# Neighbourhood attention in an encoder layer: key chunks of 16 columns moved by 8, two for each query block

## The chip, the cores and the metric

The kernel runs on one core of one Trainium2 chip. Its time is the device time of one execution in microseconds (us). The time before is the median of three runs.

A core has five engines that run side by side, each with its own instruction stream: TensorE (PE in the profile; its weight loads stand apart as PEld), VectorE (DVE), ScalarE (ACT), GpSimd (POOL) and SyncE (SP). They wait for each other through semaphores. TensorE computes `out = weights^T @ moving`: a weight load brings 128 x 128 values into the array, and a matmul streams the columns of the moving operand past them and adds into a bank of PSUM of 128 x 512 float32 values.

## What is computed

One encoder layer on 512 tokens of width 2048, in float32. One projection gives queries, keys, values and gates for 32 heads of 64 dimensions. Sixteen heads (group A) do dilated sliding-window attention, which the change leaves alone. Sixteen heads (group B) do neighbourhood attention. Both are gated, concatenated, projected, added to the residual and normalised.

For group B the 512 tokens are a grid of 8 rows by 64 columns. With 8 rows the window covers all of them, and along the columns it is 16 wide, around the query and clamped at the grid's edges:

```
q_start = np.clip(qcol - NA_COLS // 2, 0, GRID_W - NA_COLS)
col_mask = (kcol >= q_start[:, :, None]) & (kcol < q_start[:, :, None] + NA_COLS)
bias = jnp.where(col_mask[:, None, :, None, :], bias, NEG_INF)
s = jnp.einsum('bhrqd,bhrkd->bhrqk', q_blk, k_blk).astype(jnp.float32) * scale + bias_blk[None]
p = jax.nn.softmax(s, axis=-1)
return jnp.einsum('bhrqk,bhrkd->bhrqd', p, v_blk.astype(jnp.float32))
```

Queries are taken in four blocks of 16 columns (128 queries with the 8 rows). The queries of columns 0 to 15 need key columns 0 to 23; those of 16 to 31 need 8 to 39; those of 32 to 47 need 24 to 55; those of 48 to 63 need 40 to 63.

## The kernel before, in words

**Precision.** Each float32 operand is split into a high part and a low remainder (ACT writes the high part, DVE subtracts), and a product is made of two or three matmuls that add into one bank.

**Stages.** First come six gate products and the splitting of the input. Then six blocks of Strassen products give keys, queries and values of both groups, which are stored in DRAM. While these run, POOL builds the tables of biases in DRAM (`prep_heads` for group A, `prep_b` for group B, there the learned bias and the column mask together). Then comes the attention stage (in the profile about 561 to 900 us), and last the rest of the output projection with the normalisation.

**The attention stage** is one loop of 136 steps whose order on PE, ACT, DVE and SP is written out by hand; POOL's order is left to a scheduler. Step n belongs to query block n % 4 of head n // 4. Heads come in pairs, pairs of group A and of group B in turn, so eight steps (an octet) are one pair. A step does this:

- `scores(n)` (L548, L549): two matmuls with the block's 128 queries (high part with half of a remainder, then the rest) as weights and the keys as the moving operand. DVE adds the bias and takes the row's extreme (L512, `softmax`), and ACT takes the exponential into a tile `p` (L516). The tiles `p` are a ring of three.
- `turn(n - 2)` (L566): PE transposes the probabilities of two steps before, 128 keys at a time. Each transpose loads 128 columns of `p` as weights and streams an identity of 128 columns. ACT copies the result as the high part `th` (L572), DVE makes the low part `tl` (L573).
- at n % 4 = 2, `values(n // 4 - 1)` (L586): the previous head's probabilities, high and low, are multiplied with its values, for which four chunks of 128 keys lie in the tile `vv`. Then ACT copies one half and DVE adds both (L707, L708).
- between these, `fill` issues a fixed number of matmuls of other work: gate products (L459), and then the first half of the output projection (L635). In all there are 864 of them in the stage, whatever the heads do.

**Group B before.** The values lie in chunks of 16 columns by 8 rows: chunk 0 is columns 0 to 15, and so on. Query block b uses the chunks b - 1, b and b + 1 that exist: two at the edges, three in the middle. So scores are 256 or 384 columns wide, `turn` makes two or three transposes, and `values` runs, for each of `th` and `tl`, over chunk 1 for 384 queries, chunk 2 for 384, chunk 0 for 256 and chunk 3 for 256. For `th` chunk 2 is cut in 128 and 256 queries.

**POOL in the attention stage** issues transfers only: the gate's result (L466), and for each pair the softmax denominators on their way through DRAM (`share`): one write `rc_d` (L601) and, when it has landed, two reads `rc` (L603).

Of the kernel before, what the change touches and what calls it, by code (L numbers as in the profile page):

```python
# [9 lines left out]
AF = mybir.ActivationFunctionType  # L10
# [38 lines left out]
def _col_masks():  # L49
    m = np.full((3, 16, 48), BIG, np.float32)  # L50
    for cq in range(16):
        for v, (q0, k0, w) in enumerate(((0, 0, 32), (16, 0, 48), (48, 32, 32))):
            lo = min(max(q0 + cq - 8, 0), 48)
            for j in range(w):
                if lo <= k0 + j < lo + 16:
                    m[v, cq, j] = 0.0
    return np.ascontiguousarray(np.repeat(m.transpose(1, 0, 2), 8, axis=0))


def _view(t, offset, dims):  # L60
    return bass.AP(tensor=t.tensor, offset=t.offset + offset, ap=dims)
# [2 lines left out]
BLOCKS = (("k", 0), ("q", 0), ("v", 0), ("k", 1), ("q", 1), ("v", 1))  # L64
ORDER = [(m % 2, m // 2) for m in range(2 * PAIRS)]
EARLY = 6
BIAS = ((0, 32), (256, 48), (640, 32))
BW = 896


def hybrid_layer(tc, xT, xn, w_in, w_early, w_gate, w_out, t5x, brow, rpb, cmask, eye, gain, lbias, out):
    nc = tc.nc
    from contextlib import ExitStack
    with ExitStack() as ctx:
# [8 lines left out]
        def f(ap):  # L83
            return ap.bitcast(F32)
# [51 lines left out]
        v_d = [dram.tile([PAIRS, 128, 4, 256], F32, name=f"v{g}_d") for g in range(2)]  # L136
# [24 lines left out]
        def prep_b(g):  # L161

            held = []

            def rows():
                b0 = slot("b0", F32, "rpbs")
                r = b0[:, :720].rearrange("p (d j) -> p d j", d=15)
                masks = b0[:, 720:864].rearrange("p (v j) -> p v j", v=3)
                held.extend((r, masks))
                nc.gpsimd.dma_start(masks, cmask)  # L170
                for c in range(16):
                    nc.gpsimd.dma_start(r[8 * c:8 * c + 8],
                                      _view(rpb, PADB + 8 * g * RPB - 1 + c * (RPBW - 1), [[RPB, 8], [31, 15], [1, 48]]))

            def table(v):
                r, masks = held
                w, o = BIAS[v][1], 16 if v == 0 else 0
                gt = slot("b1", F32, "gt")[:, :15 * w].rearrange("p (d j) -> p d j", d=15)
                nc.gpsimd.tensor_tensor(gt, masks[:, v:v + 1, 0:w].to_broadcast([128, 15, w]), r[:, :, o:o + w],
                                        ALU.subtract)  # L180
                held.append(gt.rearrange("p d j -> p (d j)"))

            def write(v):
                at, w = BIAS[v]
                for k in range(8):
                    nc.gpsimd.dma_start(_view(bias_d[1], (1024 * g + 16 * k) * BW + at, [[BW, 16], [128 * BW, 8], [1, 8 * w]]),
                                      held[2][:, w * (7 - k):w * (7 - k) + 8 * w])
                held.pop()

            def both(v):  # L190
                write(v - 1)
                table(v)

            return [rows, lambda: None, lambda: table(0), lambda: both(1), lambda: both(2), lambda: write(2)]


# [3 lines left out]
        for tag, n, ops in (("s0", 4, A5), ("s1", 4, A5), ("c0", 2, A6), ("c1", 2, A6),  # L200
                            *((f"n{i}", 1, A6) for i in range(4)), *((f"n{i}", 1, A3) for i in range(4, 12))):
            t = slot(tag, F32R, "op").rearrange("p (n s q) -> p n s q", n=n, s=2)
# [286 lines left out]

        def load_v(i):  # L490

            g, j = ORDER[i]
            vv = slot(f"t{4 * (i % 2) + 2}", F32R, "vv").rearrange("p (b e) -> p b e", b=4)
            nc.sync.dma_start(f(vv.rearrange("p b e -> p (b e)")), v_d[g][j].rearrange("p b e -> p (b e)"))
            vs[i] = vv.rearrange("p b (h e) -> p b h e", h=2)

        def load_sg(i):
            sgs[i] = sg_ring.next("sg")
            nc.sync.dma_start(sgs[i], sg_d[i])

        def softmax(sc, bias, n, grp, i, col):

            s = s_ring.next("s")
            p = p_ring.next("p")
            mn = small.tile([128, 1], F32, name="mn", tag="mn")
            if col == 0:
                dens[i] = small.tile([128, 8], F32, name="den", tag="den")
            den = dens[i][:, col:col + 1]
            flat = (s[:, :n], sc[:, :n])
            if grp == 1:  # L510
                flat = (t.rearrange("p (r c) -> p r c", r=8) for t in flat)
            nc.vector.tensor_tensor_reduce(*flat, bias, 1.0, 3e38, ALU.add, ALU.min, mn)  # L512
            order = "p (r b c) -> p b r c"

            def exponent():
                nc.scalar.activation(p[:, :n].rearrange("p (b r c) -> p b r c", r=8, c=16),  # L516
                                     s[:, :n].rearrange(order, r=8, c=16), AF.Exp, bias=mn, scale=-1.0, accum_out=den)
            return p, exponent

        SLOT = ((0, 2), (1, 3, 5), (4, 6, 8), (7, 9))  # L520
        loaded, vs, biases, probs, turned, dens, sgs, yt, rcs = {}, {}, {}, {}, {}, {}, {}, {}, {}

        def head(h):
# [4 lines left out]
        def load_bias(h):  # L528
            g, _, _, hg = head(h)
            bias = ring_b.next("bias")  # L530
            n = BW if g else 560
            nc.sync.dma_start(bias[:, :n], bias_d[g][hg])
            biases[h] = bias

        def scores(n):

            h, b = divmod(n, 4)
            g, i, a, _ = head(h)
            qt, ql, kt = loaded[i]
            cols = slice(128 * b, 128 * b + 128)  # L540
            sc = bank(pss, "sc")
            o, ko = sc, kt[:, a]
            if g:
                rows = "p (r w) -> p r w"
                c0, nch = max(b - 1, 0), 2 if b in (0, 3) else 3
                o = sc[:, :128 * nch].rearrange(rows, r=8)
                ko = ko.rearrange(rows, r=8)[:, :, c0 * 16:(c0 + nch) * 16]
            nc.tensor.matmul(o, qt[:, a, cols], ko, start=True, stop=False)  # L548
            nc.tensor.matmul(o, ql[:, a, cols], ko, start=False, stop=True)  # L549
            if g == 0:  # L550
                p, exponent = softmax(sc, biases[h][:, 48 - 16 * b:560 - 16 * b], 512, 0, i, 4 * a + b)
                probs[n] = p, 4
                return exponent
            at, w = BIAS[(0, 1, 1, 2)[b]]
            p, exponent = softmax(sc, biases[h][:, at:at + 8 * w].rearrange(rows, r=8), 128 * nch, 1, i, 4 * a + b)
            probs[n] = p, nch
            return exponent

        def turn(n):
            h, b = divmod(n, 4)  # L560
            p, nch = probs.pop(n)
            if b == 0:
                turned[h] = slot("s0", F32R, "th"), slot("s1", F32R, "tl")
            pt = bank(pst, "pt").rearrange("p (k q) -> p k q", k=4)
            for k in range(nch):
                nc.tensor.transpose(pt[:, k], p[:, k * 128:k * 128 + 128], ident)  # L566
            if head(h)[0] == 0:
                th, tl = (t.rearrange("p (k q) -> p k q", k=4)[:, :, 128 * b:128 * b + 128] for t in turned[h])
            else:
                s0 = SLOT[b][0]  # L570
                th, tl = (t.rearrange("p (s q) -> p s q", s=16)[:, s0:s0 + 2 * nch - 1:2] for t in turned[h])
            nc.scalar.activation(th, pt[:, :nch], AF.Copy)  # L572
            nc.vector.tensor_tensor(tl, pt[:, :nch], f(th), ALU.subtract)  # L573

        rest = ((0, 0, 256, 0), (3, 256, 512, 8))
        whole = ((1, 0, 384, 2), (2, 128, 512, 5)) + rest
        opening = ((1, 0, 384, 2), (2, 384, 512, 7), (2, 128, 384, 5)) + rest
        full = tuple((k, 0, 512, 4 * k) for k in range(4))

        def values(h):  # L580
            g, i, a, _ = head(h)
            vv = vs[i]
            pv = bank(pss, "pv")
            for m, (src, parts) in enumerate(zip(turned.pop(h), (opening, whole) if g else (full, full))):
                for n, (kc, q0, q1, s) in enumerate(parts):
                    nc.tensor.matmul(pv[:, q0:q1], vv[:, kc, a], src[:, 128 * s:128 * s + q1 - q0],  # L586
                                     start=m == 0 and n == 0, stop=m == 1 and n == 3)
            if a == 0:
                yt[i] = y_ring.next("y")
            me, other = slice(64 * a, 64 * a + 64), slice(64 - 64 * a, 128 - 64 * a)  # L590
            return pv[me], pv[other], yt[i][me], tmp[me]
# [90 lines left out]
        with tc.manual_schedule(engines=engines):  # L682
# [6 lines left out]
            for n in range(136):  # L689
                b, i = n % 4, n // 8  # L690
# [11 lines left out]
                exponent = scores(n) if n < 128 else None  # L702
                if mixing:
                    if exponent:
                        exponent()
                    mine, theirs, y, t = values(n // 4 - 1)
# [28 lines left out]
        for tiles, src, first in ((gb, gain, 0), (bb, lbias, 6)):  # L735
            for i in range(4):
                t = slot(f"n{first + i}", F32, "gain")
# [76 lines left out]
        for dc in (2, 3):  # L814
            for u in range(4, 8):
                raw = out_ring.next("wraw")
                nc.sync.dma_start(raw[:, :1024], w_out[8 * dc + u])
                i = 2 * (u - 4)
                wts[dc, u] = [slot(f"{'tr'[dc - 2]}{i + m}", F32R, "wlast") for m in range(2)]
                split(raw[:, :1024], *wts[dc, u])  # L820
        for t in range(4):
            for dc in (2, 3):
                acc = bank(pacc, "acc") if dc == 2 else bank((pss, pst)[t % 2], "acc")
                parts = (slice(0, 384), slice(384, 512)) if (t, dc) == (3, 3) else (slice(0, 512),)
# [69 lines left out]
```

## Time and profile before

| what | value |
|---|---|
| median of three runs | 996.21 us (996.02 to 996.49) |
| the profiled execution: its time, its span | 997.12 us, 995.3 us |
| PE busy, PEld busy | 981.0 us (99%), 866.9 us (87%) |
| DVE, ACT, POOL busy | 765.9 us (77%), 499.9 us (50%), 208.6 us (21%) |
| mean granted TensorE clock | 0.995 |
| until the first scores, 0 to 561.29 us | PE 558.22, DVE 451.20, ACT 257.00, POOL 168.23 us busy |
| 561.29 to 892.00 us (attention) | PE 330.19, DVE 236.62, ACT 220.43, POOL 29.40 us busy |
| 892.00 to 995.30 us | PE 92.61, DVE 78.09, ACT 22.47, POOL 11.00 us busy |

How it is read: the span is the time from the first to the last instruction of the profiled execution. A matmul's busy time contains its way through the array, so matmuls in a row overlap in the profile; what one costs is the distance from its start to the start of the next. The timeline merges equal instructions that follow each other into one row with their count, and a row that merges several widths names that of the first.

### The profile page before, as it was taken

To read this page: it belongs to the slowest core of one execution; us is meant where nothing else is said; L and a number is where in the kernel's file an instruction comes from. 1 tells how busy PE (TensorE), PEld (TensorE's weight loads), DVE (VectorE), ACT (ScalarE), POOL (GpSimd) and SP (SyncE) were. 2 spreads that over 40 slices of the span, in tenths; PEclk is the share of its full clock that TensorE was granted. 3 is DMA by queue.
4 is the path that set the end of the run, shared out by engine and by line. 5 is a ranking of instruction groups with operands and counts; after the bars stand their busy time and mean duration, and the time that the engine had idled before them with its cause. 6 is when DMAs were issued, how large, how long until landed. Compare 5 with 4: busy or idle time off the path is not lost.

```text
span 995.3 us, 16145 instructions
## 1 busy us (share of the span) xinstructions
PE 981.0 (99%) x5899; PEld 866.9 (87%) x5899; DVE 765.9 (77%) x1146; ACT 499.9 (50%) x839; POOL 208.6 (21%) x322
## 2 busy tenths in 40 slices
PE   9999999999999999999999999999999999999995
PEld 6889999999889999999888888888888888888885
DVE  7958779678888887787987466776776867777876
ACT  6544444345344444434454367666667676773200
POOL 1003655654753730000000001001110001000021
PEclk9999999999999999999999999999999999999998
DMA  9833688698498387439527866677668677668222
GB/s 337 281 120 67 186 282 248 170 286 221 130 280 264 128 247 242 119 105 255 146 65 234 278 196 213 186 230 225 203 184 248 196 226 220 198 212 293 85 75 95
DMA packets 115567, 198.46 MB, mean 199 GB/s; under 512 B 46287, under 2 KB 64207, under 8 KB 115488
## 3 DMA queue, kind: packets, MB, share of 16 engines
q1 hardware_dynamic: 102976, 171.87, 55.5%
q0 software_dynamic: 12512, 25.57, 9.2%
q8 instruction: 46, 0.75, 0.3%
q14 instruction: 33, 0.27, 0.1%
HBM read 150.77 MB, written 46.60 MB: 198 GB/s over the span
## 4 chain that ended last, share of the span: by engine, by line
PE 96%; DVE 1%; ACT 1%; DMA 0%; issue 0%; SPq 0%; ACTq 0%; DVEq 0%
PE acc L635 15%; PE acc L459 11%; PE acc L367 11%; PE acc L365 11%; PE acc L366 11%; PE acc L358 5%; PE acc L359 5%; PE acc L360 5%; PE pv L586 5%; PE pt L566 4%; PE sc L548 2%; PE sc L549 2%; PE acc L267 2%; PE acc L268 2%; PE acc L269 2%; PE sc L635 1%
## 5 line engine op out<-in xcount | busy, mean ns | idle before, releaser
L87 ACT ACTIVATE wh<-braw 128x1024 fp32r<-128x1024 f32 x168 | 178.0, 1060 | 237.0 <-PE acc L366 158.0
L88 DVE TENSOR_TENSOR wl<-braw,wh 128x1024 fp32r<-128x1024 f32 x168 | 206.1, 1229 | 73.8 <-ACT wh L87 72.5
L365 PE MATMUL acc<-xk,wh 128*128 128x256 f32 x512 | 143.6, 282 | 1.1 <-ACT wh L87 1.1
L366 PE MATMUL acc<-xk,wh 128*128 128x256 f32 x512 | 143.5, 282 | 0.0
L367 PE MATMUL acc<-xk,wl 128*128 128x256 f32 x512 | 141.1, 282 | 0.0
L373 DVE TENSOR_TENSOR braw<-braw 128x1024 f32<-128x1024 f32 x96 | 117.3, 1236 | 1.1
L635 PE MATMUL acc<-wh,yk 128*128 128x512 f32 x320 | 108.7, 401 | 0.0
L573 DVE TENSOR_TENSOR tl<-pt,th 128x512 fp32r<-128x512 f32 (+2 forms) x128 | 75.3, 589 | 41.9 <-ACT th L572 40.6
L365 PE MATMUL acc<-op,wh 128*128 128x256 f32 x384 | 107.4, 282 | 0.0
L366 PE MATMUL acc<-op,wh 128*128 128x256 f32 x384 | 107.4, 282 | 0.0
L516 ACT ACTIVATE p<-s,mn 128x512 f32<-128x512 f32 (+2 forms) x128 | 82.0, 640 | 49.0 <-DVE mn L512 48.6
L367 PE MATMUL acc<-op,wl 128*128 128x256 f32 x384 | 105.2, 283 | 0.0
L365 PEld LDWEIGHTS acc<-xk,wh 128*128 128x128 f32 x512 | 97.2, 190 | 1.6 <-ACT wh L87 1.5
L366 PEld LDWEIGHTS acc<-xk,wh 128*128 128x128 f32 x512 | 97.2, 190 | 0.1
L572 ACT ACTIVATE th<-pt 128x512 fp32r<-128x512 f32 (+2 forms) x128 | 65.9, 516 | 60.5 <-PE pt L566 58.9
L367 PEld LDWEIGHTS acc<-xk,wl 128*128 128x128 f32 x512 | 95.8, 190 | 0.0
L459 PE MATMUL acc<-xk,wh 128*128 128x512 f32 x320 | 90.7, 401 | 0.0
L512 DVE CUSTOM_DVE_ANT_0 s<-sc,bias 128x512 f32<-128x512 f32 (+2 forms) x128 | 74.4, 581 | 15.0 <-PE sc L549 14.1
L367 PEld LDWEIGHTS acc<-op,wl 128*128 128x128 f32 x384 | 71.5, 190 | 1.7 <-DVE wl L88 1.7
L365 PEld LDWEIGHTS acc<-op,wh 128*128 128x128 f32 x384 | 73.0, 190 | 0.0
L366 PEld LDWEIGHTS acc<-op,wh 128*128 128x128 f32 x384 | 73.0, 190 | 0.0
L566 PEld LDWEIGHTS pt<-ident,p 128*128 128x128 f32 x416 | 53.1, 140 | 16.1
(156 smaller groups left out, 2058.7 us busy)
## 6 DMA issues: line engine op xcount, KB each, us to landing
braw<-in_w_in SPq DMA_DIRECT2D x96, 512.0 KB, 5.0
wraw<-in_w_out SPq DMA_DIRECT2D x32, 512.0 KB, 6.2
wraw<-in_w_gate SPq DMA_DIRECT2D x20, 512.0 KB, 5.3
k_d<-kst SPq DMA_DIRECT2D x64, 128.0 KB, 4.4
q_d<-kst SPq DMA_DIRECT2D x64, 128.0 KB, 3.5
v_d<-vst SPq DMA_DIRECT2D x32, 256.0 KB, 5.0
q<-q_d SPq DMA_DIRECT2D x32, 256.0 KB, 6.1
k<-k_d SPq DMA_DIRECT2D x16, 512.0 KB, 5.4
```

Of the source, the lines that this page charges most:

```text
L87: nc.scalar.activation(hi, raw, AF.Copy)
L88: nc.vector.tensor_tensor(lo, raw, f(hi), ALU.subtract)
L365: nc.tensor.matmul(o, h[:, c], ah, start=k == 0 and n == 0, stop=False)
L366: nc.tensor.matmul(o, h[:, c], al, start=False, stop=False)
L367: nc.tensor.matmul(o, l[:, c], ah, start=False, stop=k == 7 and n == 1)
L373: nc.vector.tensor_tensor(dst[u], dst[u], other[u], ALU.add)
L459: nc.tensor.matmul(acc, w[:, k * 128:k * 128 + 128], X[8 * u + k][:, s], start=u == 0 and n == 0 and k == 0, stop=u == 1 and n == 2 and k ...
L512: nc.vector.tensor_tensor_reduce(*flat, bias, 1.0, 3e38, ALU.add, ALU.min, mn)
L516: nc.scalar.activation(p[:, :n].rearrange("p (b r c) -> p b r c", r=8, c=16), s[:, :n].rearrange(order, r=8, c=16), AF.Exp, bias=mn, scale ...
L566: nc.tensor.transpose(pt[:, k], p[:, k * 128:k * 128 + 128], ident)
L573: nc.vector.tensor_tensor(tl, pt[:, :nch], f(th), ALU.subtract)
L635: nc.tensor.matmul(acc[:, part], yk[k][:, s, c], w[:, wk], start=first and kk == 0 and n == 0, stop=last and kk == 1 and n == 2)
```

## The change

For group B, the chunks of values now hold 16 columns that begin at column 8: chunk 0 is columns 8 to 23, chunk 1 is 24 to 39, chunk 2 is 40 to 55, and chunk 3 is columns 56 to 63 and 0 to 7. Each query block then needs exactly two chunks. The scores are computed for the columns that the block needs, 24, 32, 32 and 24, which with 8 rows are 192, 256, 256 and 192 columns in place of 256, 384, 384 and 256. At the edges the quarter of `p` that belongs to columns the block doesn't see is set to zero on POOL. The tables of biases shrink with the scores (896 to 640 values for each query). The values of group B are loaded by three transfers for a pair in place of one. In `values` both halves run over five matmuls, of 256, 128, 256, 256 and 128 queries.

```diff
-        for v, (q0, k0, w) in enumerate(((0, 0, 32), (16, 0, 48), (48, 32, 32))):
+        for v, (q0, k0, w) in enumerate(((0, 0, 24), (16, 8, 32), (48, 40, 24))):
...
-BIAS = ((0, 32), (256, 48), (640, 32))
-BW = 896
+BIAS = ((0, 24), (192, 32), (448, 24))
+BW = 640
...
-                w, o = BIAS[v][1], 16 if v == 0 else 0
+                w, o = BIAS[v][1], 16 if v == 0 else 8
...
         def load_v(i):
-            nc.sync.dma_start(f(vv.rearrange("p b e -> p (b e)")), v_d[g][j].rearrange("p b e -> p (b e)"))
+            if g == 0:
+                nc.sync.dma_start(f(vv.rearrange("p b e -> p (b e)")), v_d[g][j].rearrange("p b e -> p (b e)"))
+            else:
+                at = j * 128 * 1024
+                for p0, c0, n, col, blk in ((0, 0, 4, 8, 0), (64, 0, 3, 0, 1), (64, 3, 1, 0, 0)):
+                    nc.sync.dma_start(f(vv[p0:p0 + 64, c0:c0 + n].rearrange("p b e -> p (b e)")),
+                                      _view(v_d[g], at + 1024 * col + 256 * blk,
+                                            [[16 * 1024, 8], [1024, 8], [1, 256 * n]]))
...
-            order = "p (r b c) -> p b r c"
+            order, c = "p (r b c) -> p b r c", 8 if grp else 16
             def exponent():
-                nc.scalar.activation(p[:, :n].rearrange("p (b r c) -> p b r c", r=8, c=16),
-                                     s[:, :n].rearrange(order, r=8, c=16), AF.Exp, bias=mn, scale=-1.0, accum_out=den)
+                nc.scalar.activation(p[:, to:to + n].rearrange("p (b r c) -> p b r c", r=8, c=c),
+                                     s[:, :n].rearrange(order, r=8, c=c), AF.Exp, bias=mn, scale=-1.0, accum_out=den)
...
+        COLS = ((0, 24), (8, 32), (24, 32), (40, 24))
...
         def scores(n):
-                c0, nch = max(b - 1, 0), 2 if b in (0, 3) else 3
-                o = sc[:, :128 * nch].rearrange(rows, r=8)
-                ko = ko.rearrange(rows, r=8)[:, :, c0 * 16:(c0 + nch) * 16]
+                c0, w = COLS[b]
+                o = sc[:, :8 * w].rearrange(rows, r=8)
+                ko = ko.rearrange(rows, r=8)[:, :, c0:c0 + w]
...
+            if w == 24:
+                none = 0 if b == 0 else 192
+                nc.gpsimd.memset(p[:, none:none + 64], 0.0)
+            probs[n] = p, 2
...
         def turn(n):
-                s0 = SLOT[b][0]
-                th, tl = (t.rearrange("p (s q) -> p s q", s=16)[:, s0:s0 + 2 * nch - 1:2] for t in turned[h])
+                th, tl = (t[:, 256 * b:256 * b + 256].rearrange("p (k q) -> p k q", k=2) for t in turned[h])
...
-        rest = ((0, 0, 256, 0), (3, 256, 512, 8))
-        whole = ((1, 0, 384, 2), (2, 128, 512, 5)) + rest
-        opening = ((1, 0, 384, 2), (2, 384, 512, 7), (2, 128, 384, 5)) + rest
+        near = ((0, 0, 256, 128), (3, 0, 128, 0), (2, 256, 512, 640), (1, 128, 384, 384), (3, 384, 512, 896))
```

On PE, at the third query block of the second head of a B pair, the instructions stood like this before (scores `sc` of that block, then the values product `pv` of the pair's first head):

```order
L548 MATMUL sc<-k,q 128x384
L549 MATMUL sc<-k,ql 128x384
L586 MATMUL pv<-th,vv 128x384
L586 MATMUL pv<-th,vv 128x128
L586 MATMUL pv<-th,vv 128x256 x3
L586 MATMUL pv<-tl,vv 128x384 x2
L586 MATMUL pv<-tl,vv 128x256 x2
```

And with the change they stand like this at the same place:

```order
L556 MATMUL sc<-k,q 128x256
L557 MATMUL sc<-k,ql 128x256
L596 MATMUL pv<-th,vv 128x256
L596 MATMUL pv<-th,vv 128x128
L596 MATMUL pv<-th,vv 128x256 x2
L596 MATMUL pv<-th,vv 128x128
L596 MATMUL pv<-tl,vv 128x256
L596 MATMUL pv<-tl,vv 128x128
L596 MATMUL pv<-tl,vv 128x256 x2
L596 MATMUL pv<-tl,vv 128x128
```

The scores become narrower, and the values product goes from nine matmuls to ten, four of them 128 wide in place of one. The fillers between keep their places.

On POOL, in the second pair of group B (pair 3 of 0 to 15), there stands with the change (before, only the rows `sg_d`, `rc_d` and `rc` stood there; `p` is the tile of probabilities):

```order
L466 DMA sg_d<-sgo 128x512
L567 MEMSET p 128x64
L611 DMA rc_d<-tmp 8x128
L567 MEMSET p 128x64
L613 DMA rc<-rc_d 64x512 x2
L567 MEMSET p 128x64
L466 DMA sg_d<-sgo 128x512
L567 MEMSET p 128x64
```

Four fills a pair (blocks 0 and 3 of two heads) now stand in POOL's stream between the transfers, 32 in all. In pairs 1 and 13 the second fill stands behind both `rc` instead of ahead of them. On SP three `vv` transfers stand for one in each pair of group B.

More of the change, by code (lines that the diff above doesn't have):

```diff
@@ L499, in load_sg, with softmax @@
             nc.sync.dma_start(sgs[i], sg_d[i])
-        def softmax(sc, bias, n, grp, i, col):
+        def softmax(sc, bias, n, grp, i, col, to=0):
             s = s_ring.next("s")
@@ L512, in softmax @@
             nc.vector.tensor_tensor_reduce(*flat, bias, 1.0, 3e38, ALU.add, ALU.min, mn)
-            order = "p (r b c) -> p b r c"
+            order, c = "p (r b c) -> p b r c", 8 if grp else 16
             def exponent():
-                nc.scalar.activation(p[:, :n].rearrange("p (b r c) -> p b r c", r=8, c=16),
-                                     s[:, :n].rearrange(order, r=8, c=16), AF.Exp, bias=mn, scale=-1.0, accum_out=den)
+                nc.scalar.activation(p[:, to:to + n].rearrange("p (b r c) -> p b r c", r=8, c=c),
+                                     s[:, :n].rearrange(order, r=8, c=c), AF.Exp, bias=mn, scale=-1.0, accum_out=den)
             return p, exponent
-        SLOT = ((0, 2), (1, 3, 5), (4, 6, 8), (7, 9))
+        COLS = ((0, 24), (8, 32), (24, 32), (40, 24))
         loaded, vs, biases, probs, turned, dens, sgs, yt, rcs = {}, {}, {}, {}, {}, {}, {}, {}, {}
@@ L553, in scores @@
                 return exponent
-            at, w = BIAS[(0, 1, 1, 2)[b]]
-            p, exponent = softmax(sc, biases[h][:, at:at + 8 * w].rearrange(rows, r=8), 128 * nch, 1, i, 4 * a + b)
-            probs[n] = p, nch
+            at = BIAS[(0, 1, 1, 2)[b]][0]
+            p, exponent = softmax(sc, biases[h][:, at:at + 8 * w].rearrange(rows, r=8), 8 * w, 1, i, 4 * a + b,
+                                  64 if b == 0 else 0)
+            if w == 24:
+                none = 0 if b == 0 else 192
+                nc.gpsimd.memset(p[:, none:none + 64], 0.0)
+            probs[n] = p, 2
             return exponent
@@ L569, in turn @@
             else:
-                s0 = SLOT[b][0]
-                th, tl = (t.rearrange("p (s q) -> p s q", s=16)[:, s0:s0 + 2 * nch - 1:2] for t in turned[h])
+                th, tl = (t[:, 256 * b:256 * b + 256].rearrange("p (k q) -> p k q", k=2) for t in turned[h])
             nc.scalar.activation(th, pt[:, :nch], AF.Copy)
             nc.vector.tensor_tensor(tl, pt[:, :nch], f(th), ALU.subtract)
-        rest = ((0, 0, 256, 0), (3, 256, 512, 8))
-        whole = ((1, 0, 384, 2), (2, 128, 512, 5)) + rest
-        opening = ((1, 0, 384, 2), (2, 384, 512, 7), (2, 128, 384, 5)) + rest
-        full = tuple((k, 0, 512, 4 * k) for k in range(4))
+        near = ((0, 0, 256, 128), (3, 0, 128, 0), (2, 256, 512, 640), (1, 128, 384, 384), (3, 384, 512, 896))
+        full = tuple((k, 0, 512, 512 * k) for k in range(4))
         def values(h):
@@ L583, in values @@
             pv = bank(pss, "pv")
[L584 to L587, printed above, removed]
+            parts = near if g else full
+            for m, src in enumerate(turned.pop(h)):
+                for n, (kc, q0, q1, at) in enumerate(parts):
+                    nc.tensor.matmul(pv[:, q0:q1], vv[:, kc, a], src[:, at:at + q1 - q0],
+                                     start=m == 0 and n == 0, stop=m == 1 and n == len(parts) - 1)
             if a == 0:
```

## The prediction

> **What bounds the kernel now.** I read the page's first two parts and its chain first, to see which engine ends the time; then the stretches of single octets, to see whether that holds where the change is; then the waits of the attention stage; and last PE's timeline, for the price of each instruction.
>
> ```profile
> PE 981.0 (99%) x5899; PEld 866.9 (87%) x5899; DVE 765.9 (77%) x1146; ACT 499.9 (50%) x839; POOL 208.6 (21%) x322
> PEclk9999999999999999999999999999999999999998
> PE 96%; DVE 1%; ACT 1%; DMA 0%; issue 0%; SPq 0%; ACTq 0%; DVEq 0%
> ```
>
> PE is busy for 981.0 of 995.3 us at the full granted clock, and 96% of the chain that ended last is PE. In single octets of the attention stage (a pair of group A at 731.70, of group B at 624.83 and 752.91; columns: us, then busy time of PE, PEld, DVE, ACT, POOL) it looks like this:
>
> ```profile
> 624.83:645.33 20.50, 20.50 (x113) 17.39 (x111) 13.72 (x34) 13.06 (x31) 2.16 (x4) 1.00 0.75 216
> 731.70:752.91 21.21, 20.96 (x111) 17.22 (x109) 15.71 (x34) 14.38 (x31) 2.15 (x4) 1.00 0.77 217
> 752.91:771.60 18.69, 18.69 (x104) 15.89 (x103) 13.15 (x34) 13.05 (x31) 1.57 (x3) 1.00 0.80 229
> ```
>
> In a B octet PE has no idle time, DVE is busy 13.15 of 18.69 us and ACT 13.05, so 5 us of either are free. PE's own waits from 560 to 905 us (total, times, longest) are next to nothing:
>
> ```profile
> PEld sc L548 <- DVE mn L512: 1.2, 3, 0.5
> PEld pv L586 <- ACT th L572: 0.6, 2, 0.4
> PE sc L548 <- DVE mn L512: 0.5, 2, 0.3
> ```
>
> So time taken out of PE's stream in B octets should come out of the kernel, nearly one for one, as long as nothing new holds PE up. The fillers are a fixed number of matmuls in a fixed order; they shrink no further and fill no gap by themselves.
>
> **The price of one instruction on PE.** A busy time holds the pipeline's length, so I take distances of starts, in one B octet:
>
> ```profile
> 752.91 0.28 PE L548 MATMUL sc<-k,q 128*128 128x256 f32 x1
> 753.03 0.28 PE L549 MATMUL sc<-k,ql 128*128 128x256 f32 x1
> 753.14 0.39 PE L635 MATMUL acc<-wl,yk 128*128 128x512 f32 x1
> ...
> 755.44 0.34 PE L548 MATMUL sc<-k,q 128*128 128x384 f32 x1
> 755.61 0.34 PE L549 MATMUL sc<-k,ql 128*128 128x384 f32 x1
> 755.79 0.39 PE L635 MATMUL acc<-wh,yk 128*128 128x512 f32 x1
> ...
> 758.30 1.07 PE L586 MATMUL pv<-th,vv 128*128 128x512 f32 x4
> 759.21 1.07 PE L586 MATMUL pv<-tl,vv 128*128 128x512 f32 x4
> ...
> 760.35 0.38 PE L566 MATMUL pt<-ident,p 128*128 128x128 f32 x2
> 760.49 0.37 PE L548 MATMUL sc<-k,q 128*128 128x256 f32 x1
> 760.69 0.28 PE L549 MATMUL sc<-k,ql 128*128 128x256 f32 x1
> ...
> 767.73 0.80 PE L586 MATMUL pv<-th,vv 128*128 128x384 f32 x5
> 768.37 0.75 PE L586 MATMUL pv<-tl,vv 128*128 128x384 f32 x4
> 768.96 0.40 PE L635 MATMUL acc<-wh,yk 128*128 128x512 f32 x1
> ```
>
> 512 columns: 0.91 / 4 = 0.228 us. 384: 0.35 / 2 = 0.175. 256: 0.23 / 2, about 0.117. These lie on one line of 0.00043 us a column, 0.111 for 256 columns. Transposes don't: two of them and the 256-wide score behind them take 0.34 us (760.35 to 760.69); less 0.117 that is 0.11 each, although they stream only 128 columns, for which the line gives 0.06. The values product says the same. Its second half (two of 384, two of 256) takes 0.59, which is the sum of the single prices, 0.584. Its first half has the same 1280 columns in five matmuls and takes 0.64: the 128-wide one costs 0.64 - 0.175 - 3 x 0.117 = 0.11. So every instruction with its own load of 128 x 128 weights costs at least about 0.11 us, and **below some 240 columns narrowing buys nothing.** This decides two terms of the sum.
>
> **The sum, part by part.** There are 16 heads in group B.
>
> Middle scores: 2 blocks x 2 matmuls x 16 = 64 go from 384 to 256 columns: 64 x (0.175 - 0.117) = 3.7 us.
>
> Edge scores: 64 go from 256 to 192. No row shows 192. By the line it would be 0.117 - 64 x 0.00043 = 0.089, by the floor 0.11. The gain is between 0 and 64 x 0.028 = 1.8 us; I take the floor, which two kinds of row show: 64 x 0.007 = 0.4 us.
>
> Transposes: each middle block needs one less, 32 in all, at 0.11: 3.5 us. Here the floor works for the change, as each transpose removed takes a whole weight load with it.
>
> Values product: 1.23 us before. After, each half is three of 256 and two of 128: by the floor 3 x 0.117 + 2 x 0.11 = 0.57, together 1.15: 0.08 less, 16 x 0.08 = 1.3 us. By columns alone (0.06 for 128) it would be 0.94 and 4.6 us; if a 128-wide one cost 0.13, nothing would be left. I take 1.2 us.
>
> The Trainium skill, page "TensorE: Matmul & The Clock Gate", section "Back-to-back issue gap", gives about 81 ns for each matmul of 128 columns in a stream of weight loads and matmuls. By that rule a values product would take about 1.03 us and the sum would be some 2 us larger; the row above, with 0.11 us, disagrees.
>
> PE in all: 3.7 + 0.4 + 3.5 + 1.2 = **8.8 us less**, 0.55 us for each head and 1.1 for each B octet.
>
> The fills on POOL are new. Their price on POOL has no row; the nearest is the fill of 64 x 1024:
>
> ```profile
> L474 POOL MEMSET ql<- 64x1024 f32 x2 | 1.9, 952 | 180.3 <-DVE vst L220 162.4 <-DVE wl L88 17.9
> POOL rc L603 <- DMA rc_d<-tmp: 42.2, 10, 6.0
> 837.61 0.52 POOL L601 DMA_DIRECT2D rc_d<-tmp  x1 [14.28 <-ACT tmp L600]
> 842.89 1.05 POOL L603 DMA_DIRECT2D rc<-rc_d  x2 [4.76 <-DMA rc_d<-tmp]
> 845.09 0.38 PE L566 MATMUL pt<-ident,p 128*128 128x128 f32 x2
> ```
>
> A sixteenth of its columns should take between 0.06 and 0.95 us; I take 0.2, since POOL has been idle over 16 us of each B octet. What matters is who waits. The transposes of an edge block now wait for POOL too, two steps after its scores. POOL works in order, and a fill that stands behind `rc` waits for the landing of `rc_d`. The worst place is pair 13, where the second fill is behind both `rc`: they would end at 842.89 + 1.05 = 843.94, the fill at 844.1, and the transposes that need it start at 845.09 (block 3 of the first head). That leaves 1.0 us. Elsewhere only the third fill is behind `rc`, a step later. I cost the waits at nothing; the cover is these steps, and without it a longest `rc_d` wait of 6.0 us would hold PE up for about 0.3 us, once or twice. The further wait on the instruction itself costs the sequencer something like this row, which PE's queue hid so far:
>
> ```profile
> L548 PEldq EVENT_SEMAPHORE  x31: 51/51/51, 557.2 to 868.9; - x31
> ```
>
> Unhidden on all 32 blocks, that would be 1.6 us, the bound on the side of a loss.
>
> DVE and ACT get less to do, which keeps them behind PE as they were:
>
> ```profile
> L573 DVE TENSOR_TENSOR tl<-pt,th 128x384 fp32r<-128x384 f32 x32 | 17.7, 553 | 6.3 <-ACT th L572 6.1
> L512 DVE CUSTOM_DVE_ANT_0 s<-sc,bias 128x384 f32<-128x384 f32 x32 | 17.5, 546 | 2.9 <-PE sc L549 2.6
> L573 DVE TENSOR_TENSOR tl<-pt,th 128x256 fp32r<-128x256 f32 x32 | 13.4, 420 | 10.6 <-ACT th L572 10.4
> L512 DVE CUSTOM_DVE_ANT_0 s<-sc,bias 128x256 f32<-128x256 f32 x32 | 13.3, 415 | 0.0
> ```
>
> For each middle block DVE saves 0.13 + 0.13 us, for each edge block half of 0.13 on the scores: about 32 x 0.26 + 32 x 0.07 = 10.6 us, 1.3 for an octet against PE's 1.1. ACT saves alike with its exponentials and copies. The exponential now gathers runs of 8 values in place of 16, which no row prices; ACT's 5 free microseconds in an octet cover even 0.3 us on each of eight.
>
> The loads: three `vv` transfers for one, 16 more on SP, with the same bytes; a transfer is issued half a pair before the values are needed, so it is hidden. The bias tables give 448 KB to 320 KB for each head. POOL's table building before 561 us shrinks; PE doesn't wait for it. All this at nothing.
>
> **How that makes a time.** The profiled execution took 997.12 us (span 995.3), 0.91 more than the median of the three runs, 996.21. Less 8.8 its span would be 986.5, its time 988.3, and the median 987.4.
>
> **The rivals.** First, *no floor for narrow matmuls*: edge scores and 128-wide values cost their columns alone, 3.7 + 1.8 + 3.5 + 4.6 = 13.6 us less, 982.6. For it: 192 was never seen. Against it: the transposes and the 128-wide row, both at 0.11. Chance 6%.
>
> Second, *DVE or ACT takes over*: the A octet at 731.70 already shows 0.25 us of PE idle, and its steps follow a B octet that now ends sooner. If each B pair gave half of its 1.1 us back there, the gain would be 4.4 us and the time 991.8; if all, no change. Against it: DVE's work in a B octet falls by more than PE's. Chance 7%.
>
> Third, on the other side, *POOL's stream stops PE*: a fill behind a transfer comes too late, at transposes which stand in PE's order with everything else behind them. A pair gains 1.1 us, so the kernel turns slower once each pair loses more. With the 6.0 us wait in every pair and the fill late by 1.5 us, 8 x 1.5 = 12 us are lost, and the time is 999.4. Against it: the 1.0 us of room at the worst place, two or more elsewhere. Chance 4%.
>
> That the change doesn't do what it says is excluded by the order of instructions: the widths and counts above are in it.
>
> **How the numbers follow.** The forecast, 987.4 us, has 83%. Its own range goes from the edge scores at their columns and a little of the values (gain 11.7, 984.5) to no gain from either plus 1.6 us of semaphores (7.2 - 1.6 = 5.6, 990.6). I give 984.5 to 991.0, which leaves out the first and third rival and most of the second. A measurement of this kernel tells about 0.2%, 2 us, from no change. Faster: the forecast, the first rival, and some of the second, 92%. Same: the rest of the second and part of the third, 5%. Slower: 3%.
>
> **What would show it.** In the profile after, from one start to the next: transposes still 0.11, the middle scores 0.117, the edge scores 0.11 (0.09 would show that there is no floor at that width), the values product 1.15. A B octet near 624 us takes 19.4 us, one of the second kind 17.6; A octets stay at 20.7 to 22.5. PE has no new waits on POOL. The forecast is wrong if PE's idle time in the stage grows beyond a microsecond or two, with DVE, ACT or a fill as its cause, or if A octets become longer.

## The result, and the profile after

The changed kernel takes **987.49 us** (median of five runs, 987.20 to 987.91) against 996.21 us before: a ratio of 0.9909, with a 95% interval of 0.9899 to 0.9920. That is 8.7 us less; the prediction was 8.8 us less, 987.4 us. Beside other kernels on another occasion the same kernel took 988.57 us against 996.38 us before (0.9922, interval 0.9909 to 0.9934), so about 1 us is the limit of what comparisons between occasions can tell.

The profiled execution has a span of 985.4 us, 9.9 us less than before. The page's first part and its chain:

```profile
PE 971.5 (99%) x5883; PEld 858.3 (87%) x5883; DVE 756.0 (77%) x1146; ACT 491.6 (50%) x839; POOL 207.6 (21%) x354
PE 95%; DVE 1%; ACT 1%; issue 1%; DMA 1%; POOL 0%; SPq 0%; ACTq 0%; POOLq 0%
```

PE lost 9.5 us of busy time and still ends everything. Of the span's 9.9 us, 1.4 us have nothing to do with the change: they lie ahead of the first scores (561.29 us before, 559.90 after), and there within the first 29 us, long before POOL builds a table (the same matmul of the first products, L268, starts at 28.05 us before and at 26.70 after). 1.0 us of them is the first transfer of weights, which the chains of waits show, in order of time, before and after:

```profile
2.14 4.78 DMA wraw<-in_w_early
```

```profile
2.12 3.76 DMA wraw<-in_w_early
```

In the profiles of the experiments this transfer took up to 5.56 us in code that none of them touches. So spans are best compared from the first scores on: 434.0 us before, 425.5 after, 8.5 less.

The stretches of single octets after (a B pair, an A pair, a B pair; the same pairs as in the prediction; columns: us, busy time of PE, PEld, DVE, ACT, POOL, then granted clock and DMA):

```profile
622.40:642.07 19.67, 19.67 (x110) 16.50 (x109) 12.91 (x34) 12.19 (x31) 2.62 (x7) 1.00 0.75 218
726.45:747.38 20.93, 20.73 (x110) 17.05 (x109) 15.33 (x34) 14.23 (x31) 2.30 (x5) 1.00 0.80 204
747.38:765.20 17.82, 17.82 (x102) 15.02 (x101) 12.07 (x34) 12.15 (x31) 2.04 (x6) 1.00 0.83 242
```

The B octets went from 20.50 and 18.69 to 19.67 and 17.82 us and are filled by PE as before. The A octet went from 21.21 to 20.93.

PE's timeline in the second of these B octets shows the prices (two edge scores, transposes, two middle scores, the values product of a B head, and the fillers behind them):

```profile
756.91 0.25 PE L556 MATMUL sc<-k,q 128*128 128x192 f32 x1
757.00 0.27 PE L557 MATMUL sc<-k,ql 128*128 128x192 f32 x1
757.11 0.42 PE L645 MATMUL acc<-wh,yk 128*128 128x512 f32 x1
757.37 0.39 PE L645 MATMUL acc<-wl,yk 128*128 128x512 f32 x1
...
758.07 0.38 PE L578 MATMUL pt<-ident,p 128*128 128x128 f32 x2
758.20 0.47 PE L645 MATMUL acc<-wl,yk 128*128 128x512 f32 x1
758.52 0.63 PE L645 MATMUL acc<-wh,yk 128*128 128x512 f32 x2
...
759.21 0.28 PE L556 MATMUL sc<-k,q 128*128 128x256 f32 x1
759.33 0.28 PE L557 MATMUL sc<-k,ql 128*128 128x256 f32 x1
759.45 0.63 PE L645 MATMUL acc<-wh,yk 128*128 128x512 f32 x2
...
761.52 0.69 PE L596 MATMUL pv<-th,vv 128*128 128x256 f32 x5
762.05 0.75 PE L596 MATMUL pv<-tl,vv 128*128 128x256 f32 x5
762.64 0.45 PE L645 MATMUL acc<-wh,yk 128*128 128x512 f32 x1
```

A pair of middle scores takes 0.24 us. A pair of edge scores takes 0.20, but the filler behind it takes 0.26 in place of 0.23, so narrowing to 192 gave almost nothing. Two transposes take 0.13 and make the filler behind them 0.09 longer: 0.11 each. The values product takes 1.12 us, and the filler behind it runs to 762.92, 0.05 more than its own time: 1.17.

PE's waits from 555 to 890 us (total, times, longest) contain one of a new kind:

```profile
PEld sc L556 <- DVE mn L520: 1.4, 4, 0.6
PE sc L556 <- DVE mn L520: 0.6, 2, 0.4
PEld pt L578 <- POOL p L567: 0.5, 1, 0.5
```

It lies in pair 13, and the timeline there shows the fill standing behind both `rc`, which had waited 5.71 us for `rc_d`, and the load of the second transpose behind the fill:

```profile
835.96 1.05 POOL L613 DMA_DIRECT2D rc<-rc_d  x2 [5.71 <-DMA rc_d<-tmp]
...
836.82 0.74 PE L578 MATMUL pt<-ident,p 128*128 128x128 f32 x2
...
837.00 0.25 POOL L567 MEMSET p<- 128x64 f32 x2
837.23 0.14 PEld L578 LDWEIGHTS pt<-ident,p 128*128 128x128 f32 x1 [0.49 <-POOL p L567]
```

### The profile page after: what moved, and what is told of

Read it like the earlier page. It is cut to its first block, busy times and chain, and to the rows that moved or that the text cites. A ratio compares the mean times of both kernels' runs of the same rounds, so it can differ in the third digit from the quotient of the medians.

```text
span 985.4 us, 16207 instructions
## 1 busy us (share of the span) xinstructions
PE 971.5 (99%) x5883; PEld 858.3 (87%) x5883; DVE 756.0 (77%) x1146; ACT 491.6 (50%) x839; POOL 207.6 (21%) x354
## 4 chain that ended last, share of the span: by engine, by line
PE 95%; DVE 1%; ACT 1%; issue 1%; DMA 1%; POOL 0%; SPq 0%; ACTq 0%; POOLq 0%
PE acc L645 14%; PE acc L459 11%; PE acc L367 11%; PE acc L365 11%; PE acc L366 11%; PE acc L358 5%; PE acc L359 5%; PE acc L360 5%; PE pv L596 4%; PE pt L578 4%; PE acc L267 2%; PE acc L268 2%; PE acc L269 2%; PE sc L556 2%; PE sc L557 2%; PE sc L645 1%
## 5 line engine op out<-in xcount | busy, mean ns | idle before, releaser
L584 DVE TENSOR_TENSOR tl<-pt,th 128x256 fp32r<-128x256 f32 (+1 forms) x128 | 71.1, 555 | 44.8 <-ACT th L583 43.5
L524 ACT ACTIVATE p<-s,mn 128x512 f32<-128x512 f32 (+2 forms) x128 | 76.8, 600 | 51.1 <-DVE mn L520 50.6
L583 ACT ACTIVATE th<-pt 128x256 fp32r<-128x256 f32 (+1 forms) x128 | 62.4, 490 | 58.1 <-PE pt L578 55.9
L520 DVE CUSTOM_DVE_ANT_0 s<-sc,bias 128x512 f32<-128x512 f32 (+2 forms) x128 | 68.0, 531 | 14.6 <-PE sc L557 14.2
L645 PEld LDWEIGHTS acc<-wh,yk 128*128 128x128 f32 x320 | 58.5, 189 | 8.9
```

The source lines that it names most:

```text
L524: nc.scalar.activation(p[:, to:to + n].rearrange("p (b r c) -> p b r c", r=8, c=c), s[:, :n].rearrange(order, r=8, c=c), AF.Exp, bias=mn, ...
L645: nc.tensor.matmul(acc[:, part], yk[k][:, s, c], w[:, wk], start=first and kk == 0 and n == 0, stop=last and kk == 1 and n == 2)
```

## The experiments

All are edits of the changed kernel. Each was timed in four or five runs (one in eleven) beside the kernel before, whose median stayed between 996.3 and 996.6 us. Where I compare with the changed kernel on another occasion I take the middle of its two medians, 988.0 us, give or take 0.6; the octets of the profiles, and the time from the first scores to the end (425.5 us in the changed kernel's first profile), tell more.

### Middle scores over 384 columns again

```diff
                 c0, w = COLS[b]
-                o = sc[:, :8 * w].rearrange(rows, r=8)
-                ko = ko.rearrange(rows, r=8)[:, :, c0:c0 + w]
+                k0, wide = ((0, 24), (0, 48), (16, 48), (40, 24))[b]
+                o = sc[:, :8 * wide].rearrange(rows, r=8)
+                seen = o[:, :, c0 - k0:c0 - k0 + w]
+                ko = ko.rearrange(rows, r=8)[:, :, k0:k0 + wide]
```

DVE then reads `seen` in place of the whole.

> The changed kernel, but PE computes the middle blocks' scores over 384 columns again (64 matmuls); DVE, ACT and all else read and do what they do in the changed kernel. The forecast's theory (PE ends the time, a matmul costs its columns or the 0.11 us of the next weight load, whichever is more): 64 x 0.058 = 3.7 us back, so 991.2 us against 987.5. If DVE or ACT ended the time of the B octets, the wider matmuls would be partly hidden: under 989.5 us.

Measured: 990.94 us (990.67 to 992.64), ratio 0.9949 (0.9935 to 0.9963). The B octet near 623 us:

```profile
623.29:643.42 20.13, 20.13 (x110) 16.97 (x109) 13.09 (x34) 12.18 (x31) 2.62 (x7) 1.00 0.71 213
```

It is 0.46 us longer than the 19.67 of the changed kernel, and eight matmuls at 0.058 make 0.46. PE's time comes through whole there; DVE and ACT hide none of it. In two of the B octets less comes through, 0.28 and 0.16 us: there the changed kernel has PE waiting, for DVE (from 664.62 us) and for a fill (pair 13, shown above), and the wider matmuls take up part of these waits. From the first scores on the profile is 3.1 us longer than the changed kernel's (428.6 us against 425.5), and the median is 2.9 above 988.0, in place of 3.7.

### Edge scores over 256 columns again

```diff
+                k0, wide = ((0, 32), (8, 32), (24, 32), (32, 32))[b]
```

(the rest as above).

> The changed kernel, but PE computes the edge blocks' scores over 256 columns again (64 matmuls); all else as changed. With a floor of one weight load at 0.11 to 0.117 us the width between 192 and 256 is free: 987.5 to 987.9 us. If a narrow matmul costs its columns alone (0.089 us for 192), 64 x 0.028 = 1.8 us come back: 989.3 us.

Measured: 988.33 us (987.91 to 989.33), ratio 0.9921 (0.9908 to 0.9933). The B octet:

```profile
623.47:643.14 19.67, 19.67 (x110) 16.55 (x109) 12.91 (x34) 12.18 (x31) 2.62 (x7) 1.00 0.74 218
```

It is as long as with 192 columns. The width between 192 and 256 is all but free: the floor holds, and columns alone would have made this octet 0.22 us longer. The B octets from 748.5 and 786.9 us are 0.1 us longer (17.90 and 17.89, against 17.82 and 17.77), about what the forecast's 0.4 us in all would give.

### The third transpose again

```diff
+            if nch == 2 and b in (1, 2):
+                nc.tensor.transpose(pt[:, 2], p[:, 0:128], ident)
```

> The changed kernel with a third transpose for each middle block again (32 more on PE, into a part of the bank that nobody reads); ACT and DVE copy two chunks as changed. By the price from the trace (0.11 us, a weight load): 32 x 0.11 = 3.5 us back, 991.0 us. By its 128 streamed columns alone (0.06 us): 1.9 us, 989.4 us.

Measured: 991.11 us (990.21 to 991.99), ratio 0.9946 (0.9933 to 0.9958). The A octet ahead and the B octet:

```profile
600.96:623.39 22.43, 22.43 (x119) 18.64 (x118) 15.81 (x32) 14.44 (x31) 2.89 (x6) 1.00 0.77 204
623.39:643.40 20.01, 20.01 (x114) 16.84 (x112) 13.04 (x34) 12.19 (x31) 2.62 (x7) 1.00 0.72 215
```

Three of a pair's four added transposes fall into the B octet (19.67 to 20.01, 0.11 each); the fourth, which is turned two steps later, falls into the A octet that follows a B pair (22.30 in the changed kernel, 0.13 more). A transpose costs 0.11 us here, not the 0.06 of its 128 columns. From the first scores on the profile is 2.8 us longer than the changed kernel's (428.3 us).

### Chunk 3 in one matmul

```diff
-        near = ((0, 0, 256, 128), (3, 0, 128, 0), (2, 256, 512, 640), (1, 128, 384, 384), (3, 384, 512, 896))
+        near = ((0, 0, 256, 128), (2, 256, 512, 640), (1, 128, 384, 384), (3, None, None, None))
...
+                    if q0 is None:
+                        o = pv.rearrange("p (b q) -> p b q", b=4)[:, 0:4:3]
+                        x = src.rearrange("p (k q) -> p k q", k=16)[:, 0:8:7]
...
```

> The changed kernel with the two 128-wide matmuls of chunk 3 joined into one of 2 x 128 columns in each half of the values product: eight matmuls in place of ten, the same columns. With the floor each half falls from 3 x 0.117 + 2 x 0.11 to 4 x 0.117 us: 0.10 less, 32 halves, 3.3 us in all, 984.2 us. If a narrow matmul costs its columns alone (two of 128: 0.12, one of 256: 0.117), nothing changes: 987.4 us.

Measured: 986.72 us (985.82 to 987.05), ratio 0.9901 (0.9887 to 0.9914). PE's timeline of a values product:

```profile
762.32 0.64 PE L601 MATMUL pv<-th,vv 128*128 128x256 f32 x4
762.79 0.64 PE L601 MATMUL pv<-tl,vv 128*128 128x256 f32 x4
763.27 0.40 PE L650 MATMUL acc<-wh,yk 128*128 128x512 f32 x1
763.51 0.38 PE L578 MATMUL pt<-ident,p 128*128 128x128 f32 x2
```

It takes 0.95 us in place of 1.17 with the same columns: the price of a narrow matmul is as the floor says. But of the 3.3 us that this takes off PE's stream the medians show only 0.8 to 1.9, and the profile 2.3 from the first scores on (423.3 us against 425.5), 0.4 of which is the wait for a fill in pair 13, which this profile doesn't have. PE's waits on DVE in the attention stage grew from 1.4 to 2.0 us (its weight loads' row), in A octets, where the scores wait for a bank that DVE has yet to read:

```profile
PEld sc L556 <- DVE mn L520: 2.0, 3, 0.8
...
PE sc L556 <- DVE mn L520: 1.3, 3, 0.6
```

The A octet from 727 to 748 us takes 21.15 us, 0.2 more than without the edit. DVE there has a weight's low part (1.22 us) and the low part of the gated output (0.69 us) ahead of the scores.

### The changed kernel unaltered

> The changed kernel unaltered, beside the next three on the same chip: 987.5 us, less than 0.3 us from its first measurement against the same kernel before.

Measured: 988.57 us (987.73 to 989.97), ratio 0.9922 (0.9909 to 0.9934): 1.1 us more than at first. My expectation of 0.3 us was too narrow. Its profile's span is 1.5 us longer than the first: 0.6 us of that lies ahead of the first scores and 0.8 behind 864 us, where PE waited once for a weight's low part from DVE; between them only the octet of pair 13 differs by over 0.05 us. It was on the chip together with three others: each fill eight times, no fill, and the last experiment below.

### Each fill eight times

```diff
-                nc.gpsimd.memset(p[:, none:none + 64], 0.0)
+                for _ in range(8):
+                    nc.gpsimd.memset(p[:, none:none + 64], 0.0)
```

> The changed kernel with each fill of zeros on POOL made eight times (256 in place of 32, 0.15 us each), which puts most of each pair's second fill behind the two reads rc in every B pair. If fills reach PE only where one stands behind the rc_d wait (seen once, in pair 13, for 0.5 us), the eight pairs now lose between 0 and 1 us each: 988.5 to 993 us, with PE's waits on POOL L567 making up the difference. If POOL's stream never matters to PE, 987.5 us.

Measured: 991.66 us (989.87 to 992.35), 3.1 us more than the changed kernel beside it. PE's waits:

```profile
PEld pt L579 <- POOL p L568: 3.8, 3, 2.2
...
PE pt L579 <- POOL p L568: 2.9, 2, 1.8
```

Only three of the eight pairs waited, but one for 2.2 us, more than the 1 us that I had allowed a pair. Whether a fill is late hangs on when `rc_d` lands. And a wait costs more than its length. This is the stretch around the longest, in pieces of 2 us (granted clock in the third column from the end):

```profile
798.50:800.50 2.00, 0.68 (x4) 0.28 (x2) 0.52 (x3) 0.00 (x0) 1.20 (x4) 1.00 1.02 393
800.50:802.50 2.00, 1.50 (x5) 1.21 (x6) 0.42 (x1) 1.14 (x4) 1.28 (x11) 0.77 0.98 362
802.50:804.50 2.00, 2.00 (x11) 1.99 (x10) 0.43 (x2) 1.77 (x4) 0.00 (x0) 0.50 0.34 94
804.50:806.50 2.00, 2.00 (x13) 1.74 (x13) 0.69 (x2) 0.98 (x2) 0.52 (x4) 0.88 0.00 0
```

After the pause PE's clock was granted at 0.50 for some 3.4 us: by the clocks in these rows, 0.9 us of the second stretch, the whole third and 0.5 us of the fourth. This octet took 21.39 us against 17.77 in the changed kernel's first profile: 3.6 us for a pause of about 2.

### No fill

```diff
-                nc.gpsimd.memset(p[:, none:none + 64], 0.0)
+                pass
```

> The changed kernel without the fills of zeros: the quarter of the edge blocks' probabilities that should be zero keeps what an earlier block left there, so this part of the computation is left out. If the fills cost only the one wait seen in pair 13: 987.0 us. If the further semaphore on 32 transposes costs PE's sequencer 0.05 us each as well: 985.4 us.

Measured: 987.72 us (987.20 to 988.18), 0.85 us less than the changed kernel beside it, 0.9911 (0.9898 to 0.9925). The octet of pair 13 took 17.79 us, and 18.32 in the profile of the unaltered kernel beside it: 0.5 us, the one wait. So the fills cost about that, and the semaphores on 32 transposes cost PE nothing that shows. The 0.3 us beyond are within the scatter.

### Tables and their loads as before

```diff
-BIAS = ((0, 24), (192, 32), (448, 24))
-BW = 640
+BIAS = ((0, 32), (256, 48), (640, 32))
+BW = 896
...
-            p, exponent = softmax(sc, biases[h][:, at:at + 8 * w].rearrange(rows, r=8), 8 * w, 1, i, 4 * a + b,
+            p, exponent = softmax(sc, biases[h][:, at:at + 8 * wide].rearrange(rows, r=8)[:, :, skip:skip + w], 8 * w, 1, i, 4 * a + b,
```

> The changed kernel with the bias tables of before: built and stored with 896 values for each query and loaded whole (448 KB a head in place of 320), of which DVE reads the part it needs. The prediction put building and loading at nothing: 987.5 to 988.6 us, the two medians of the changed kernel. If the smaller tables are worth something (less POOL work beside DVE before 560 us, less traffic beside the weights in the attention stage), the time rises by more than 1 us.

Measured: 987.80 us (987.46 to 988.09), ratio 0.9915 (0.9901 to 0.9929). The smaller tables bring nothing that shows, neither where they are built nor where they are loaded.

### Twice the low part on DVE

```diff
             nc.vector.tensor_tensor(tl, pt[:, :nch], f(th), ALU.subtract)
+            if nch == 2:
+                nc.vector.tensor_tensor(tl, pt[:, :nch], f(th), ALU.subtract)
```

> The changed kernel with DVE's low part of the turned probabilities made twice in the B heads: 64 more operations of 0.42 us, 27 us in all, 3.4 us in each B pair, of which the profile shows over 5 us free on DVE. If PE alone ends the time there, the rise is small, at most 3 us (988 to 991.5 us), and lies in the first steps of the A pairs that follow. If DVE were about to take over in B pairs, as the second rival has it, the rise would be at least a third of the 27 us: over 996 us.

Measured: 996.66 us (995.54 to 997.83, eleven runs), ratio 1.0000 (0.9991 to 1.0009). The whole gain is gone. By its number this falls on the rival's side: about a third of the 27 us came through. Where it came through is another matter. An A octet, an A octet and the B octet behind it:

```profile
642.90:667.00 24.10, 22.92 (x119) 18.69 (x118) 18.15 (x39) 14.29 (x31) 2.31 (x5) 1.00 0.67 204
729.04:751.38 22.34, 21.18 (x110) 17.05 (x109) 17.02 (x37) 14.12 (x31) 2.31 (x5) 1.00 0.72 206
751.38:769.21 17.83, 17.83 (x103) 14.98 (x102) 13.31 (x37) 12.17 (x31) 2.05 (x6) 1.00 0.75 213
```

The B octet is as long as ever, with PE busy throughout; the A octets have grown from 22.55 and 20.93 us, with 1.2 us of PE idle in each, nearly all of it one wait of the scores for DVE. (Two other A octets, near 601 and 687 us, hardly grew.) DVE carries a backlog out of the B pair, two of whose eight added operations stand in the next octet's first steps anyway, and PE pays at the next A pair. So my reading of more than 5 us free on DVE in a B octet was wrong as cover. Of DVE's 5.75 us of idle time in the same octet of the changed kernel (747.38 to 765.20 us), 5.6 are waits for ACT. The added work used 1.2 us of it (DVE busy 12.07 us without, 13.31 with); as much and more fell into the A octet (15.33 and 17.02), where PE waits for DVE even without it.

### DVE's and POOL's order, without and with the joined matmul

Two edits of order: the low part of the gated output moves from two steps after to four; POOL joins the engines whose order is written out, and the reads `rc` are issued three steps after `rc_d`, so that two fills stand ahead of them.

```diff
-            later(2, lambda: nc.vector.scalar_tensor_tensor(t[:, 1], y, 0.5, f(t[:, 0]), op0=ALU.mult, op1=ALU.subtract))
+            later(4, lambda: nc.vector.scalar_tensor_tensor(t[:, 1], y, 0.5, f(t[:, 0]), op0=ALU.mult, op1=ALU.subtract))
...
             later(0, send)
+            later(3, fetch)
...
-        engines = {mybir.EngineType.PE, mybir.EngineType.SP, mybir.EngineType.DVE, mybir.EngineType.Activation}
+        engines = {mybir.EngineType.PE, mybir.EngineType.SP, mybir.EngineType.DVE, mybir.EngineType.Activation,
+                   mybir.EngineType.Pool}
```

Alone:

> The changed kernel with the last trial's two edits of order (the low part of the gated output two steps later on DVE; POOL's order written out, the reads rc three steps after rc_d), and the values product as changed, with 128-wide matmuls. By the stalls in the changed kernel's profile (0.5 us at the fill of pair 13, some 0.4 us each at the A pairs 8 and 14, less elsewhere) 1.2 to 1.8 us come off: about 986.5 us. Then the joined matmuls are worth the rest of the 4.4 us that the last trial gained on the changed kernel beside it, 2.6 to 3.2 us. If the edits of order bring nothing by themselves, 988 us.

Measured: 986.76 us (986.17 to 987.17), ratio 0.9903 (0.9887 to 0.9919). The A octet near 727 us and the octet of pair 13:

```profile
727.35:747.81 20.46, 20.46 (x111) 17.03 (x109) 15.33 (x34) 14.38 (x31) 2.32 (x5) 1.00 0.72 212
824.70:842.52 17.82, 17.82 (x102) 15.02 (x101) 11.99 (x33) 11.50 (x31) 2.03 (x6) 1.00 0.79 242
```

They took 20.93 and 18.19 us in the changed kernel; both waits are gone.

With the joined matmul of chunk 3:

> The changed kernel with three edits: chunk 3's two 128-wide matmuls joined (3.4 us less on PE, of which the first trial returned only 0.8, with new PE waits on DVE at the second or third step of A pairs); the low part of the gated output made on DVE two steps later, out of the way of those scores; POOL's order written out like the others', with the reads rc three steps after rc_d, so that the first two fills after it stand ahead of them. If the gain of the joined matmuls was lost to that crowding on DVE and to the fill of pair 13: 983.5 us. If it was lost to anything else: 986 to 987 us.

Measured: **984.19 us** (983.61 to 984.46), ratio 0.9877 (0.9864 to 0.9891), 4.4 us less than the changed kernel beside it. This is the fastest version here, 12.2 us below the kernel before on the same chip. By the medians the joined matmul is worth 2.6 us on top of the edits of order (984.19 against 986.76, on another occasion), where without them it showed 0.8 to 1.9. The profiles don't bear out so large a difference. From the first scores on they take 425.5 us in the changed kernel, 423.3 with the joined matmul, 424.1 with the edits of order and 421.9 with both. So the joined matmul takes off about 2.3 us either way, and the edits of order about 1.4 either way. Only if the wait of pair 13 is left out of the first comparison does the joined matmul gain more behind the edits of order, 2.3 us against 1.9. That its gain had been lost mainly to the crowding on DVE is therefore not shown.

The gain stays below the 3.3 us of PE's stream: the A octets from 801 and 840 us still take 20.93 and 21.07 us, where the one from 763 us takes 20.24. There PE's weight loads for the values product wait for ACT's copy `th`, and as long again for something that the profile doesn't show (801.15 to 860.76 us):

```profile
PEld pv L601 <- ACT th L583: 0.8, 2, 0.4
PEld pv L601 <- issue: 0.8, 2, 0.4
```

No run removes these waits, so what they cost is not shown.

## Why the prediction was right

**What bounds the kernel.** PE ends the time, and what leaves its stream in B pairs leaves the kernel: shown by the middle scores (0.46 us of 0.46 in a B octet) and by the third transpose (0.34 us for three at 0.11), in the octets where PE had no other wait.

**The sum.** Middle scores, 3.7 us forecast: the octet of the first experiment gives 8 x 0.46 = 3.7. Transposes, 3.5: the two octets of the third experiment give 8 x (0.34 + 0.13) = 3.8. Edge scores, 0.4: not more, the octet shown doesn't change and two later ones by 0.1; a pair of them with the filler behind takes 0.46 us in the changed kernel's timeline against 0.47 with 256 columns. Values product, 1.2: 1.23 before, 1.17 in the rows shown, 16 x 0.06 = 1.0. These make 8.5 to 8.9 us. The fills took back 0.4 to 0.5 of that, and 8.5 us from the first scores on was what the spans showed. Eight times an octet is the most that these experiments give: their whole profiles show 3.1 us for the middle scores and 2.8 for the transposes, because PE's other waits take up part. So each term is good to some tenths of a microsecond, and that forecast and median agree within 0.1 us is partly luck: a wait at the fills that I had put at nothing stands in it, and on the other occasion the same kernel was 7.8 us below the one before.

**The floor** was the decisive reading, and it held in both directions: it makes the 128-wide matmuls and the edge scores dear and a removed transpose worth more than its columns. What makes it is less sure. I had put it down to an instruction's own load of 128 x 128 weights. The transpose of the softmax denominators has only 8 columns of weights (128*8), and it costs as much, in the changed kernel:

```profile
752.20 0.27 PE L606 MATMUL pt<-ident,den 128*8 128x128 f32 x1
752.23 0.36 PE L556 MATMUL sc<-k,q 128*128 128x256 f32 x1
752.43 0.28 PE L557 MATMUL sc<-k,ql 128*128 128x256 f32 x1
```

It and the score behind it take 0.23 us; less 0.117 that is 0.11. So it isn't the own weights. The load of the *next* instruction's weights fits: it begins as a narrow matmul begins (at 757.02 us for the filler, behind the edge score of 757.00) and its row is 0.19 us long. A least price of some 0.11 us for any instruction fits as well, and no run separates the two. The rival without a floor, 982.6 us, is refuted by the edge scores and the joined chunk 3. Its sum had the transposes at 0.11 us like the forecast's; that price the third transpose confirms.

**The fills.** The waits for them were the term that I put at nothing. Their price on POOL, 0.2 us, was 0.15. The worst place was named rightly, pair 13; the room there was put at 1.0 us, and a wait of 5.71 us for `rc_d`, within what had been seen before, used it up and 0.5 us more. I had put 0.3 us "once or twice"; it was 0.5 once, and so my sign that PE has no new waits on POOL didn't hold. It changes from profile to profile: with the fills in the same order, the reads waited 4.74 and 4.89 us in the experiments with the third transpose and the joined matmul, and PE not at all; with the wider edge scores they waited 6.05 us, and PE 0.8. The third rival's mechanism is real, but its price left out the clock: a pause of 2 us cost 3.6.

**DVE and ACT.** The step "5 us of either are free" in a B octet was wrong as an argument. The forecast rested on it less than it seemed, because the change takes about as much from DVE (0.81 and 1.08 us in the two B octets shown) as from PE (0.83 and 0.87). With 3.4 us added to DVE in each B pair the kernel is back at 996.66 us. So DVE was close behind PE in the A octets. For a change that lightens PE alone the second rival would deserve more than 7%: of the joined matmul's 3.3 us about 1 us or more didn't come through, and PE's waits for DVE grew there.

**The tests I named.** I said 19.4 and 17.6 us for the B octets and no change in A octets. They were 19.67, 17.82 and in most A octets 0.2 us less. That was bookkeeping: a pair's last two turns and its second head's values product are issued in the next octet, so a fifth of a B pair's gain shows there.

## What to carry to other kernels

Before narrowing matmuls, find the width below which they get no cheaper: here it lies between 192 and 256 columns, at about 0.11 us for 128 x 128 float32 weights. Above it columns count, below it the number of instructions does, so drop or join instructions there.

Idle time of an engine that works in a fixed order isn't all spare capacity: look at what it waits for, and at where its backlog would be paid. When the bounding engine gets faster, look for the places where it now waits for the others: here two edits of order were worth 1.4 us more.

A small operation on a queue that also waits for transfers can have the latency of that wait (5.71 us ahead of a fill of 0.15); put it ahead of them.

## What was not expected of the hardware

A pause of TensorE of about 2 us was followed by some 3.4 us at half the granted clock (0.50 in the stretch from 802.5 us), which nearly doubled its cost. The Trainium skill, page "TensorE: Matmul & The Clock Gate", section "What's actually happening", has this half rate but puts it after an idle window of about 3.4 us; here a pause from 798.9 to 801.0 us, with one short transpose in it, was enough.

The first transfer of weights took between 3.76 and 5.56 us in profiles of kernels with the same code up to there, and moves the whole span by about as much.
